# Spacing the buffers of the main pool 2080 instead of 2048 bytes apart, 63 of them instead of 64

## The chip, the cores and the metric

The kernel runs on one core of a Trainium2 chip. The metric is the device time of one execution in microseconds (us), the median over runs. All data are float32; the matmuls of the large products read them in the float32r form.

## What is computed

One decoder layer on 512 tokens of width 2048. Cut to what matters here:

```python
mod = (silu(c) @ w_ada + b_ada)                      # six vectors: shift, scale, gate, twice
h = rmsnorm(x, g_norm_mix) * (1 + sc1) + sh1
q, k, v, xr, xg = split(h @ w_in)                    # 8 heads of 128; two LRU parts of 1024
o_attn = stick_breaking_attention(q, k, v)           # strictly causal, by log-space running sums
o_lru = rg_lru(causal_conv(xr)) * gelu(xg)
y = concat(rmsnorm(o_attn), rmsnorm(o_lru)) @ w_out
x = x + gt1 * y
h = rmsnorm(x, g_norm_mlp) * (1 + sc2) + sh2
hid = square(relu(h @ w_mlp_in))                     # 2048 -> 8192
x = x + gt2 * (hid @ w_mlp_out)                      # 8192 -> 2048
return rmsnorm(x, g_norm_final)
```

## The kernel before, in words

**Precision.** Each float32 operand of a large product is split in two: a float32r copy (high) and the difference (low). A product is then three matmuls into the same PSUM bank: high weight by high activation, high weight by low activation, low weight by high activation (`mm3`, L258 to L263; the same three written out at L1099 to L1101 and L470 to L472). ScalarE makes the high part (L244, L1063, L1069), VectorE the low part (`low`, L121 and L122).

**Operands of a matmul.** In `mm(out, w, a)` the weight tile is the stationary operand, 128x128, loaded afresh for every matmul, and the activation is the moving operand, 512 or 256 columns of 4 bytes. The value product of the attention (`v_mm`, L470 to L472) has it the other way round: the activation is stationary, and a slice of the weight tile moves.

**Stages.** (1) The projections of the recurrence (xr), while the adaLN rows are computed on VectorE from a stream of `w_ada`; (2) q, k and v, with attention, convolution, gates and scans run beside the matmuls in small steps; (3) xg, and the output projection; (4) both MLP products, as one level of a Strassen-like scheme (`strassen`, from L1080): seven products of 256-column operands per set, each 6 matmuls, with the sums of weights made by VectorE (L1057, L1064, L1065) and the sums of activations prepared ahead; (5) the last 512 output columns in plain form, and the final norm.

**What sets the order.** The program is recorded by a framework that schedules it. Priorities (`URGENT`, `EVAC` and others) and the time at which a buffer is expected to come free decide where an instruction stands on its engine, so the number of buffers of a tag takes part in the order. SyncE issues nearly all loads; GpSimd issues the stores of parts, sums and products to DRAM.

**Memory.** Tiles with a tag in `BUFS` come from one pool (`new`, L101 to L104), placed one after the other from low addresses up: constants, `ga`, then `pad` (L140; 40 columns, 160 bytes, used by nothing), `cb` (2 x 4096 bytes), `n` (5 x 2048), `a` (64 x 2048). The constants and `ga` with `pad` end at byte 19968, which is 39 times 512, and every later buffer up to the end of `a` is a multiple of 512 bytes long. So each of them starts at a multiple of 512 bytes. After `a` follow the buffers of the stages on the left side: first `wr`, `wh`, `wl`; in the MLP `w5` and `w3`. Those on the right side (`x` and `tt`; later `ts`, `raw`, `w4`) are placed from the top of the memory down. All of them also start at multiples of 512 in the kernel before.

**What lies in `a`.** Nearly all activations: x, its scaled split, hT (the normalized input, 16 pairs), q, k, v, the parts and sums of the MLP's activations, partial products on their way out, x1 and x2. In the MLP every moving operand is half of an `a` tile (256 of 512 columns), in the plain products a whole one. The weights of the first stage also lie in `a` (`weights1`). In the Strassen stages the stationary operands lie in `w3`, `w4` and `w5`.

Of the kernel before, what the change touches and what calls it, by code (L numbers as in the profile page):

```python
# [16 lines left out]
P = 128  # L17
# [23 lines left out]

URGENT = 150
EVAC = 88
PAD = 40

BUFS = {"cb": 2, "a": 64, "ga": 4, "n": 5}
COLS = {
    "wr": 512, "wh": 512, "wl": 512, "x": 1024, "cb": 1024, "tt": 1280, "n": 512, "a": 512, "ga": 4,  # L50
    "raw": 1024, "ts": 1024, "w3": 768, "w4": 1024, "w5": 1024,
# [13 lines left out]
def hybrid_layer_kernel(  # L65
# [18 lines left out]
    def stage(name):  # L84
        side, tags = STAGES[name]
        for tag in [t for t, (_, _, s) in pools.items() if s == side]:
            del pools[tag]
        region[side].close()
        pool = region[side].enter_context(tc.tile_pool(name=name, bufs=1, reuse_waits="tile", side=side))
        for tag, bufs in tags.items():  # L90
            pools[tag] = pool, bufs, side
            new(tag)
# [3 lines left out]
    count = [0]  # L96

    def T(tag, dt=F32, cols=None):
        return new(next(split_tag) if tag == "w4" else tag, dt, cols)

    def new(tag, dt=F32, cols=None):  # L101
        count[0] += 1
        pool, bufs = (sp, BUFS[tag]) if tag in BUFS else pools[tag][:2]
        return pool.tile([P, cols or COLS[tag]], dt, tag=tag, name=f"{tag}_{count[0]}", bufs=bufs)  # L104

    def bank(tag):
        count[0] += 1
# [2 lines left out]
    def const(cols, name, dt=F32):  # L110
        return sp.tile([P, cols], dt, tag=name, name=name)
# [25 lines left out]
    mods, gm1, spl = (top.tile([P, n], F32, tag=t, name=t) for n, t in ((96, "mods"), (NK, "gm1"), (HEADS, "spl")))  # L137
    region |= {side: ctx.enter_context(ExitStack()) for side in ("right", "left")}
    new("ga")
    const(PAD, "pad")  # L140
    cb = [T("cb"), T("cb")]
# [299 lines left out]
    for o in range(8):  # L441
        t = T("a")
# [805 lines left out]
    for i, (n, ps) in enumerate(parts):  # L1248
# [13 lines left out]
        if n not in left and n < NO - 1:  # L1262
# [10 lines left out]
            with tc.high_priority(offset=SETW):  # L1273
                for k, tok, q in quarters(n, *qs):
                    t = x2[k][:, tok]
# [8 lines left out]
        else:  # L1284
            with tc.high_priority(offset=SETE):
                for j, b in enumerate(bs):
                    t = T("a")
# [14 lines left out]
    for p in final:  # L1302
        t = T("a", F32R)
# [156 lines left out]
```

## Time and profile before

| | |
|---|---|
| median of 3 runs | 2049.47 us (2048.18 to 2051.11) |
| the profiled execution | 2051.77 us |
| its span, first to last instruction | 2050.1 us |
| mean granted TensorE clock | 0.995 |
| TensorE busy | 2009.6 us, 98% of the span, 14,532 matmuls |
| VectorE, ScalarE, GpSimd busy | 1764.0, 1077.8, 181.0 us |
| DMA | 441.45 MB, mean 215 GB/s |

How to read it. A matmul's duration in the profile (283 ns for 256 columns) is longer than its place in the stream, because the next one starts before it ends. What counts is the distance from start to start, called the pace here. It is read from the timeline, or from a window without idle time as its length over the number of matmuls. PE is the matmul side of TensorE, PEld its weight loads. A window's row gives, per engine, busy time and number of instructions, then the granted clock, the share of busy DMA engines and GB/s.

### The profile page before, as it was taken

How to read it: one execution, taken by the hardware profiler on the slowest of the kernel's cores; microseconds unless marked ns; L12 is line 12 of the kernel's file. 1: busy time of each engine (PE TensorE's matmuls, PEld its weight loads, DVE VectorE, ACT ScalarE, POOL GpSimd, SP SyncE). 2: the span in 40 equal slices, each digit the busy share in tenths (PEclk: the TensorE clock that was granted, in tenths of full speed). 3: DMA queues.
4: the chain of work that ended last, by engine and by line, in shares of the span. 5: the costliest groups of instructions: out<-in, count | busy, mean ns of one | idle time of the engine just before them, and what ended most of it. 6: DMA issues, size and time to landing. Idle time of an engine off the chain costs nothing.

```text
span 2050.1 us, 37927 instructions
## 1 busy us (share of the span) xinstructions
PE 2009.6 (98%) x14532; PEld 1904.8 (93%) x14532; DVE 1764.0 (86%) x2971; ACT 1077.8 (53%) x1572; POOL 181.0 (9%) x283
## 2 busy tenths in 40 slices
PE   8999999999999998999999999999999999999997
PEld 6789898778887998999999999999999999999996
DVE  8998776978888699999999999999788778778986
ACT  5443655796423575555555555456455555545542
POOL 0000000000000001221121112100011110210000
PEclk9999999999999999999999999999999999999998
DMA  9896646556789444675566656655485576667644
GB/s 363 303 326 201 200 153 203 167 172 206 226 300 325 134 156 149 213 238 182 185 217 198 194 188 220 211 191 176 148 308 207 210 254 235 232 241 248 237 148 149
DMA packets 205624, 441.45 MB, mean 215 GB/s; under 512 B 20353, under 2 KB 41985, under 8 KB 205442
## 3 DMA queue, kind: packets, MB, share of 16 engines
q1 hardware_dynamic: 178642, 360.78, 53.7%
q0 software_dynamic: 21760, 71.32, 8.9%
q10 hardware_dynamic: 5040, 6.93, 1.0%
q8 instruction: 114, 1.87, 0.4%
q14 instruction: 68, 0.56, 0.1%
HBM read 375.25 MB, written 63.70 MB: 214 GB/s over the span
## 4 chain that ended last, share of the span: by engine, by line
PE 57%; DVE 2%; DMA 1%; issue 0%; ACT 0%; SPq 0%; DVEq 0%
PE ps_mm L1101 9%; PE ps_mm L1100 9%; PE ps_mm L1099 9%; PE ps_z L1101 7%; PE ps_z L1100 7%; PE ps_z L1099 7%; PE ps_o L1101 2%; PE ps_o L1099 2%; PE ps_o L1100 2%; DMA raw<-in_w_mlp_out_dram 1%; DMA a<-x 0%; DVE w L122 0%; DMA a<-sum 0%; DVE a L1346 0%; DVE a L1276 0%
## 5 line engine op out<-in xcount | busy, mean ns | idle before, releaser
L1101 PE MATMUL ps_mm<-a,w 128*128 128x256 f32 x1696 | 479.6, 283 | 1.1 <-DVE w L122 1.1
L1100 PE MATMUL ps_mm<-a,w 128*128 128x256 f32 x1696 | 479.8, 283 | 0.0
L1099 PE MATMUL ps_mm<-a,w 128*128 128x256 f32 x1696 | 479.2, 283 | 0.0
L1063 ACT ACTIVATE w<-raw 128x768 fp32r<-128x768 f32 x244 | 204.9, 840 | 379.0 <-PE ps_mm L1100 165.6
L122 DVE TENSOR_TENSOR w<-ts,w 128x1024 fp32r<-128x1024 f32 x244 | 298.0, 1221 | 116.9 <-PE ps_mm L1100 61.6
L1101 PE MATMUL ps_z<-a,w 128*128 128x256 f32 x1304 | 369.5, 284 | 6.2 <-DVE w L122 6.2
L1099 PE MATMUL ps_z<-a,w 128*128 128x256 f32 x1304 | 369.3, 284 | 0.0
L1100 PE MATMUL ps_z<-a,w 128*128 128x256 f32 x1304 | 369.2, 284 | 0.0
L1101 PEld LDWEIGHTS ps_mm<-a,w 128*128 128x128 f32 x1696 | 325.5, 192 | 1.4 <-DVE w L122 1.4
L1100 PEld LDWEIGHTS ps_mm<-a,w 128*128 128x128 f32 x1696 | 325.7, 192 | 0.2 <-DVE a L122 0.2
L1099 PEld LDWEIGHTS ps_mm<-a,w 128*128 128x128 f32 x1696 | 325.5, 192 | 0.1
L1069 ACT ACTIVATE w<-ts 128x1024 fp32r<-128x1024 f32 x244 | 258.2, 1058 | 113.4 <-DVE ts L1065 101.9
L122 DVE TENSOR_TENSOR w<-raw,w 128x768 fp32r<-128x768 f32 (+1 forms) x296 | 267.4, 904 | 34.3 <-ACT w L244 23.4
L1101 PEld LDWEIGHTS ps_z<-a,w 128*128 128x128 f32 x1304 | 250.6, 192 | 7.1 <-DVE w L122 7.0
L1099 PEld LDWEIGHTS ps_z<-a,w 128*128 128x128 f32 x1304 | 250.8, 192 | 0.1
L1100 PEld LDWEIGHTS ps_z<-a,w 128*128 128x128 f32 x1304 | 250.7, 192 | 0.1
L244 ACT ACTIVATE wh<-wr 128x512 fp32r<-128x512 f32 (+1 forms) x184 | 113.0, 618 | 152.2 <-PE ps_mm L262 65.8
L259 PE MATMUL ps_mm<-a,wh 128*128 128x512 f32 x448 | 176.2, 393 | 3.1 <-ACT wh L244 1.4
L263 PE MATMUL ps_mm<-a,wl 128*128 128x512 f32 x448 | 175.1, 391 | 0.4 <-DVE wl L122 0.2
L262 PE MATMUL ps_mm<-a,wh 128*128 128x512 f32 x448 | 174.7, 390 | 0.0
L1057 DVE TENSOR_TENSOR ts<-raw 128x512 f32<-128x512 f32 x244 | 166.6, 683 | 3.5 <-DMA raw<-in_w_mlp_out_dram 2.4
L122 DVE TENSOR_TENSOR wl<-wr,wh 128x512 fp32r<-128x512 f32 (+1 forms) x184 | 123.7, 675 | 33.3 <-ACT wh L244 32.8
(332 smaller groups left out, 4167.0 us busy)
## 6 DMA issues: line engine op xcount, KB each, us to landing
raw<-in_w_mlp_out_dram SPq DMA_DIRECT2D x124, 512.0 KB, 4.0
raw<-in_w_mlp_in_dram SPq DMA_DIRECT2D x120, 512.0 KB, 3.9
x<-in_w_adaT_dram SPq DMA_DIRECT2D x108, 512.0 KB, 5.7
wr<-in_w_in_dram SPq DMA_DIRECT2D x160, 256.0 KB, 3.4
tt<-in_w_adaT_dram SPq DMA_DIRECT2D x52, 512.0 KB, 6.5
part<-a POOLq DMA_DIRECT2D x84, 256.0 KB, 3.9
a<-part SPq DMA_DIRECT2D x84, 256.0 KB, 6.0
prod<-a POOLq DMA_DIRECT2D x63, 256.0 KB, 5.9
```

The lines of the kernel that those rows point to most:

```text
L122: tt(out=out, in0=full, in1=f32(high), op=ALU.subtract)
L244: act(h[:, :n], r[:, :n], AF.Copy)
L259: first = mm(out, wh, ah, start=start, stop=False, **kw)
L262: mm(out, wh, al, start=False, stop=False, **kw)
L263: mm(out, wl, ah, start=False, stop=stop, **kw)
L1057: tt(out=t[:, : 2 * HT].rearrange("p (a b) -> p a b", a=2), in0=r[:, HT : 3 * HT].rearrange("p (a b) -> p a b", a=2), in1=r[:, q_(0)].unsq ...
L1063: act(h, r[:, HT:], AF.Copy)
L1069: act(h, t, AF.Copy)
L1099: mm(out, wh[:, blk(i)], ah, start=st, stop=False, **kw)
L1100: mm(out, wh[:, blk(i)], al, start=False, stop=False, **kw)
L1101: mm(out, wl[:, blk(i)], ah, start=False, stop=j == js[-1], **kw)
```

## The change

A buffer of the tag `a` is made 8 columns (32 bytes) longer, and only its first columns are handed out; there are 63 of them instead of 64.

```diff
-PAD = 40
+PAD, SKEW = 40, 8
...
-BUFS = {"cb": 2, "a": 64, "ga": 4, "n": 5}
+BUFS = {"cb": 2, "a": 63, "ga": 4, "n": 5}
...
     def new(tag, dt=F32, cols=None):
         count[0] += 1
         pool, bufs = (sp, BUFS[tag]) if tag in BUFS else pools[tag][:2]
-        return pool.tile([P, cols or COLS[tag]], dt, tag=tag, name=f"{tag}_{count[0]}", bufs=bufs)
+        n = cols or COLS[tag]
+        t = pool.tile([P, n + SKEW * (tag == "a")], dt, tag=tag, name=f"{tag}_{count[0]}", bufs=bufs)
+        return t[:, :n] if tag == "a" else t
```

2080 is 4 x 512 + 32, so the k-th buffer starts at 32k modulo 512: all sixteen multiples of 32 occur, each in 3 or 4 buffers. 63 x 2080 = 131,040 bytes, 32 fewer than 64 x 2048 = 131,072. The buffers that follow on the left side (`wr`, `wh`, `wl`; `w5`, `w3`) therefore all start at 480 modulo 512. `x`, `tt`, `ts`, `raw` and `w4` stay where they were, at multiples of 512, as do `cb` and `n` below `a`.

The line numbers of the new kernel are 2 higher from `new` on. Each engine has as many instructions as before. In a handful of places the order changes, since a buffer of `a` is expected at another time.

ScalarE, where the attention of the third pair of heads starts (`tt_770` is the score tile of its first head; `a_801` and `a_805` are the convolution's outputs, `wh_...` high parts of weights). Before:

```order
L552 ACTIVATE a_782_3879<-a_252_1034,vec_63 128x512
L552 ACTIVATE a_801_3990<-a_253_1036,vec_63 128x512
L552 ACTIVATE a_805_4015<-a_254_1038,vec_63 128x512
L244 ACTIVATE wh_787_3893<-wr_786_3891 128x512
L635 ACTIVATE tt_770_3801<-ps_z_767_3786 128x512
L635 ACTIVATE tt_770_3801<-ps_z_768_3787 128x512
L635 ACTIVATE tt_770_3801<-ps_z_769_3788 128x256
L636 ACTIVATE tt_770_3801<-tt_770_3801 128x1280
```

Now:

```order
L554 ACTIVATE a_782_3879<-a_252_1034,vec_63 128x512
L637 ACTIVATE tt_770_3801<-ps_z_767_3786 128x512
L554 ACTIVATE a_801_3990<-a_253_1036,vec_63 128x512
L246 ACTIVATE wh_787_3893<-wr_786_3891 128x512
L637 ACTIVATE tt_770_3801<-ps_z_768_3787 128x512
L246 ACTIVATE wh_793_3942<-wr_792_3940 128x512
L637 ACTIVATE tt_770_3801<-ps_z_769_3788 128x256
L554 ACTIVATE a_805_4015<-a_254_1038,vec_63 128x512
```

The first step of the scores moved ahead of two of the three convolution steps, and a weight's high part came between. VectorE and TensorE are reordered around the same place, with the same instructions.

SyncE, late in the MLP's second product (`a_3824` to `a_3827` are the four residual tiles of output group 1, `n_...` the stored combination of the last group, `raw_...` weights). Before, where the third of the four is loaded:

```order
L1270 DMA a_3824_23287<-x1_4_6544 128x512
L1270 DMA a_3825_23289<-x1_5_6545 128x512
L1270 DMA a_3826_23291<-x1_6_6546 128x512
L1055 DMA raw_3804_23117<-in_w_mlp_out_dram 128x2x512
L1055 DMA raw_3810_23173<-in_w_mlp_out_dram 128x2x512
```

Now, where it stands, after eight more weight loads:

```order
L1057 DMA raw_3865_23565<-in_w_mlp_out_dram 128x2x512
L1301 DMA n_3904_23832<-y_0_15805 128x512
L1301 DMA n_3905_23833<-y_1_15806 128x512
L1272 DMA a_3826_23291<-x1_6_6546 128x512
L1301 DMA n_3906_23834<-y_2_15807 128x512
L1272 DMA a_3827_23293<-x1_7_6547 128x512
L1301 DMA n_3907_23835<-y_3_15808 128x512
```

The third residual tile is loaded ten places later, two ahead of the fourth, and the weight loads that followed it moved up.

## The prediction

> **What bounds the kernel now.** I read the page first, then the stretches of the span as windows, then the timeline of TensorE.
>
> ```profile
> span 2050.1 us, 37927 instructions
> PE 2009.6 (98%) x14532; PEld 1904.8 (93%) x14532; DVE 1764.0 (86%) x2971; ACT 1077.8 (53%) x1572; POOL 181.0 (9%) x283
> ...
> PE 57%; DVE 2%; DMA 1%; issue 0%; ACT 0%; SPq 0%; DVEq 0%
> ```
>
> TensorE is busy for 98% of the span, and it is nearly alone in the chain that ended last. A busy share does not say how fast the matmuls follow each other, so the windows come next.
>
> ```profile
> core 0: us, PE busy (x) PEld busy (x) DVE busy (x) ACT busy (x) POOL busy (x), PEclk, DMA share, GB/s
> 0.00:80.00 80.00, 70.91 (x290) 55.83 (x291) 70.51 (x141) 37.83 (x60) 1.03 (x6) 1.00 0.98 360
> 360.00:400.00 40.00, 37.52 (x169) 30.42 (x168) 37.21 (x64) 29.16 (x46) 0.00 (x0) 0.96 0.58 179
> 560.00:600.00 40.00, 40.00 (x178) 33.11 (x177) 39.93 (x76) 13.78 (x23) 0.00 (x0) 1.00 0.81 266
> 840.00:1880.00 1040.00, 1040.00 (x8662) 1039.50 (x8661) 916.78 (x1479) 546.64 (x720) 140.31 (x226) 1.00 0.63 212
> 1960.00:1980.00 20.00, 18.85 (x157) 18.65 (x156) 17.52 (x29) 12.13 (x19) 0.00 (x0) 1.00 0.60 190
> 2006.00:2050.00 44.00, 30.51 (x228) 28.29 (x226) 31.37 (x70) 11.11 (x24) 0.00 (x0) 0.88 0.48 163
> ```
>
> From 840 to 1880 us, half of the kernel, TensorE does not idle at all at full clock: 8,662 matmuls of 256 columns in 1040.00 us, 0.1201 us each. The wide ones (512 columns, 560 to 600 us) fill 40 us with 177, so 0.226 us each. The difference, 0.106 us for 256 more columns, is 0.414 ns a column, and what a matmul takes beyond its columns is 0.1201 - 0.106 = 0.014 us, the same for both widths. Over 14,532 matmuls that fixed part is 203 us. In such stretches neither DMA (0.63) nor VectorE (917 of 1040 us) sets the time. Only the pace does, and one nanosecond on every matmul is 14.5 us, 0.7% of the kernel.
>
> **What the change can touch.** It removes one buffer of 64, adds no instruction, and moves the addresses of `a` and of what follows it on the left side.
>
> ```profile
> L1101 PE MATMUL ps_mm<-a,w 128*128 128x256 f32 x1696 | 479.6, 283 | 1.1 <-DVE w L122 1.1
> L1101 PE MATMUL ps_z<-a,w 128*128 128x256 f32 x1304 | 369.5, 284 | 6.2 <-DVE w L122 6.2
> L1101 PE MATMUL ps_o<-a,w 128*128 128x256 f32 x416 | 118.0, 284 | 0.4 <-DVE w L122 0.4
> L259 PE MATMUL ps_mm<-a,wh 128*128 128x512 f32 x448 | 176.2, 393 | 3.1 <-ACT wh L244 1.4
> L470 PE MATMUL ps_mm<-wh,a 128*128 128x256 f32 x128 | 36.5, 285 | 0.3 <-DVE a L460 0.3
> ```
>
> Each of these lines stands for one of three matmuls of the split. The Strassen stages alone read `a` as the moving operand 3 x (1696 + 1304 + 416) = 10,248 times, the plain wide products on `ps_mm` 3 x 448 = 1,344 times. Fifteen of sixteen such reads will start off a multiple of 512 bytes, where now none does. A read of 256 columns is 1024 bytes long: from an aligned start it covers exactly two pieces of 512 bytes, from any other start it touches three. The stationary operands in `w3` and `w5` move too, all to 480 modulo 512, those in `w4` stay at 0. In L470 it is `wh` and `wl` that move, at one offset, 480, not sixteen.
>
> **The pace.** No read in the trace of before starts off a multiple of 512, so the price is bounded by the places where the pace departs from 0.120 and 0.226 us without a semaphore in sight.
>
> ```profile
> 1414.39 0.28 PE L1101 MATMUL ps_mm<-a,w 128*128 128x256 f32 x1
> 1414.51 0.28 PE L1099 MATMUL ps_mm<-a,w 128*128 128x256 f32 x1
> ...
> 1415.34 0.28 PE L1100 MATMUL ps_mm<-a,w 128*128 128x256 f32 x1
> 1415.46 0.37 PE L1099 MATMUL ps_z<-a,w 128*128 128x256 f32 x1
> ```
>
> Here, after a wait, nine matmuls start within 1.07 us, 0.1189 us each: 1.1 ns less than the steady pace. So part of the 14 ns is not a law of the array; it depends on how the streams stand to each other in time.
>
> ```profile
> 289.77 0.40 PE L259 MATMUL ps_o<-tt,a 128*128 128x512 f32 x1
> 290.01 0.40 PE L262 MATMUL ps_o<-tt,a 128*128 128x512 f32 x1
> 290.25 0.40 PE L263 MATMUL ps_o<-tt,a 128*128 128x512 f32 x1
> ...
> 291.00 0.29 PE L259 MATMUL ps_o<-tt,a 128*128 128x256 f32 x1
> 291.13 0.28 PE L262 MATMUL ps_o<-tt,a 128*128 128x256 f32 x1
> ```
>
> And here, where widths change, wide ones stand 0.24 us apart (14 ns more) and a narrow one 0.13 (10 ns more), again with no wait. The price of a shifted start therefore lies between -1.1 and +14 ns a matmul by what the rows show; that the whole fixed part of 14 ns falls away is the outermost bound below. One more touched piece of 512 bytes costs nothing where the pieces are whole, since four of them carry the same fixed part as two. It can cost up to a new start, 14 ns, where the first is a fragment. I take +2 ns: nearer the locked pace, because 8,662 matmuls in a row with all their different buffers hold 0.1201 us, so the stream is robust against nearly everything, and on the positive side because a read that begins in the middle of a piece gives the array less per piece and nothing back. It is the weakest number here. The term: 14,532 x 15/16 x 2 ns = 27 us; its bounds are -15 us (-1.1 ns) and, at the slow rows, +190 us, of which I use +4 ns, 54 us, as the far end for a mean over sixteen offsets, some of which should cost nothing.
>
> The Trainium skill (TensorE: Matmul & The Clock Gate, section Back-to-back issue gap) gives a warm gap of N/2.4 + 2.5 ns, 109.2 ns for 256 columns. The trace disagrees, 120.1 ns; if the shifted starts brought the page's gap, the estimate would be 14,532 x 10.9 ns = 158 us less, 1893 us.
>
> **The DMAs of `a`.** Stores out of `a` now start at odd places of the memory, and loads land there.
>
> ```profile
> part<-a POOLq DMA_DIRECT2D x84, 256.0 KB, 3.9
> prod<-a POOLq DMA_DIRECT2D x63, 256.0 KB, 5.9
> sum<-a POOLq DMA_DIRECT2D x56, 256.0 KB, 4.2
> ```
>
> These 203 stores take 4 to 6 us each and lie in the stretch with no idle TensorE and DMA engines at 0.63: they cost nothing, and would only show if the share went near 1. In the first 80 us it is at 0.98 already, and TensorE idles 80 - 70.91 = 9.1 us. The weights loaded there land in `wr`, now at 480. Between 0 and a doubling of that idle time, +9 us, I take +1. If the DMAs were slower, the weights' buffers would come late and their splits with them.
>
> The Trainium skill (DMA: Bandwidth & Descriptors, section How a descriptor splits into AXI transactions) says that a descriptor that doesn't start 256-byte aligned needs an extra transaction. It speaks against the change; no run here shows it, and by it a row of 2048 bytes would take 9 transactions for 8, an estimate of an eighth, which the share of 0.63 absorbs.
>
> **One buffer fewer, and the order.** ScalarE's scores now go ahead of two convolution steps, and TensorE's and VectorE's rows follow. That is at about 375 us; in 360 to 400 TensorE loses 40 - 37.52 = 2.5 us, so the price is between -2.5 and about the same upward; the steps are the same and I take 0. The waiting score step is what is queued ahead on ScalarE then, with the high parts `wh` behind it. On SyncE the third residual tile of group 1 moves ten places back.
>
> ```profile
> 1966.82 4.00 DMA a<-x
> ...
> 1971.35 1.27 DVE a L1276 x3
> ...
> 1973.22 1.15 DVE w L122
> 1974.41 0.39 PE ps_mm L1101
> ```
>
> The fourth of these loads is on the chain already: it lands after 4.00 us, VectorE's in-order queue holds the residual additions (L1276) and behind them a weight's low part (L122) for which TensorE waits; 20 - 18.85 = 1.15 us are lost in that stretch. With two loads issued there instead of one it is one more landing in the worst case, +4 us, none in the best; +0.5. The last 44 us, where TensorE idles 13.5 us at short dependent steps, are not reordered on SyncE: 0.
>
> **Sum.** On the profiled execution's own time: 2051.8 + 27 + 1 + 0.5 = 2080. That execution lies 2.3 us above the median of the three runs, 2049.5, so 2078 us for the median. A measurement of this kernel can tell about 0.2%, 4 us, from no change.
>
> **The rivals.** *No effect on the pace* (chance 0.24). The steady 0.1201 us holds whatever VectorE, ScalarE and DMA do beside it, and over buffers all over the memory; if the matmul reads its operand at a rate that no start address changes, only the small terms are left: 2045.4 to 2053.6. For it: constancy. Against it: that a fixed part of 14 ns exists which is not columns, and that it is 1.1 ns smaller after a wait. The Trainium skill (SBUF — State Buffer, section Who interferes with whom) says that "PE and ACT never wait on anyone", which is this rival; the constant pace agrees with it.
>
> *Faster: the weight load and the moving operand no longer start at the same place* (0.26). Now both start at a multiple of 512 bytes, and the load of the next weights goes on beside the running matmul, from the same phase.
>
> ```profile
> L1099 PEld LDWEIGHTS ps_mm<-a,w 128*128 128x128 f32 x1696 | 325.5, 192 | 0.1
> ...
> L262 PEld LDWEIGHTS ps_mm<-a,wh 128*128 128x128 f32 x448 | 84.2, 188 | 16.1
> ```
>
> A weight load takes 192 ns beside narrow matmuls and 188 beside wide ones. If those 4 ns are a collision of two streams that meet at the same offset, sixteen offsets against two (0 and 480) would leave it in about one of sixteen or eight cases. The price is between -1.1 ns (the pace after a wait; -15 us, 2034) and -4 ns (-55 us, 1995), likeliest -2: 2022. Against it: the wide ones have the same fixed part of 14 ns without those 4 ns. VectorE does not stand in the way, 917 us of work in a stretch that would shrink to 1023. It decides from -0.3 ns on, where the gain exceeds 4 us. That most of the fixed part goes with it (up to -14 ns, -190 us, 1859) gets 0.02 of the 0.26, since no row shows a pace near 0.106 us.
>
> *The change not doing what it says*: 63 buffers 2080 bytes apart do reach all sixteen offsets, each in 3 or 4 buffers. Only the attention's value products are left out, as said. No chance of its own.
>
> **How the numbers follow.** Slower by the pace has 0.50, with +0.3 to +4 ns its own range is 2054 to 2104; its likeliest is 2078. No effect 0.24. Faster 0.26. The range 2020 to 2110 leaves out about a tenth below (the faster case beyond -2.2 ns) and a tenth above (beyond +4.3 ns, towards the slow rows). The chances of faster, same and slower are those of the three cases.
>
> **What would show it.** Right: in 840 to 1880 us fewer matmuls, about 8,530, still with no idle time, starts no longer evenly spaced but going with the buffer, and the wide ones slower by as many nanoseconds. Wrong on the sign: more than 8,662 in that window, with weight loads nearer 188 ns. Wrong on the mechanism: 0.1201 us again, and a difference, if any, in the first 80 us (DMA share, idle time), around 375 us, or at the residual loads near 1967 us.

## The result and the profile after

The changed kernel takes 2040.12 us (median of 6 runs, 2038.38 to 2043.25), the kernel before, beside it, 2049.48 us (6 runs, 2046.46 to 2053.08). The ratio is 0.9956, with a 95% interval of 0.9943 to 0.9969: faster by 0.44%, 9 us. The forecast was 2078 us, slower. The time lies in the range, since the range took in the rival "faster"; the direction was wrong.

The profiled execution took 2041.91 us with a span of 2040.2. Its page begins:

```profile
span 2040.2 us, 37961 instructions
...
PE 1997.6 (98%) x14532; PEld 1884.1 (92%) x14532; DVE 1763.7 (86%) x2971; ACT 1080.9 (53%) x1572; POOL 180.9 (9%) x283
```

TensorE has lost 12.0 us of busy time (2009.6 to 1997.6) at the same 14,532 matmuls. VectorE, ScalarE and GpSimd did not change by more than 3.1 us. The stretches, with the columns of the windows of before:

```profile
0.00:80.00 80.00, 72.52 (x292) 56.40 (x293) 71.11 (x141) 38.20 (x61) 0.94 (x6) 1.00 0.98 363
360.00:400.00 40.00, 37.98 (x171) 30.88 (x170) 37.17 (x64) 28.82 (x45) 0.00 (x0) 0.96 0.59 186
560.00:600.00 40.00, 40.00 (x174) 32.45 (x173) 39.93 (x75) 13.16 (x22) 0.00 (x0) 1.00 0.76 256
840.00:1880.00 1040.00, 1038.17 (x8772) 1036.93 (x8771) 928.40 (x1497) 554.12 (x728) 145.99 (x236) 1.00 0.64 216
1960.00:1980.00 20.00, 18.69 (x156) 18.42 (x155) 19.47 (x31) 9.32 (x12) 0.00 (x0) 1.00 0.51 171
```

Two rows carry the result, with opposite signs. In 840 to 1880 us TensorE does 8,772 matmuls of 256 columns for 8,662 before, although it now idles 1.83 us. In 560 to 600 us it does 174 where 178 stood: the wide ones have become slower. How regular the narrow ones are, the timeline of TensorE shows (start, duration):

```profile
1499.75 0.28 PE L1103 MATMUL ps_z<-a,w 128*128 128x256 f32 x1
1499.87 0.28 PE L1101 MATMUL ps_z<-a,w 128*128 128x256 f32 x1
1499.99 0.28 PE L1102 MATMUL ps_z<-a,w 128*128 128x256 f32 x1
1500.10 0.28 PE L1103 MATMUL ps_z<-a,w 128*128 128x256 f32 x1
...
1501.98 0.28 PE L1101 MATMUL ps_mm<-a,w 128*128 128x256 f32 x1
```

They stand 0.11 to 0.13 us apart, no longer an even 0.12. Taken over all starts of the trace within runs of one width (steps over 130 ns, and over 245 ns between wide ones, are left out as waits), the mean from start to start was, and is:

| | narrow, 256 columns | wide, 512 columns |
|---|---|---|
| matmuls in the program | 12,096 | 2,228 |
| before, ns | 119.90 | 227.37 |
| after, ns | 118.06 | 231.81 |
| difference x matmuls, us | -1.84: -22.3 | +4.44: +9.9 |

The two terms make -12.4 us. The spans differ by 2050.1 - 2040.2 = 9.9 us, so some 2.5 us went back into waits, most of it (1.83 us) in 840 to 1880.

### The profile page after: what moved, and what is told of

The parts are those of the page before. It is cut to its first block, busy times and chain, and to the rows that moved or that the text cites. A ratio compares the mean times of both kernels' runs of the same rounds, so it can differ in the third digit from the quotient of the medians.

```text
span 2040.2 us, 37961 instructions
## 1 busy us (share of the span) xinstructions
PE 1997.6 (98%) x14532; PEld 1884.1 (92%) x14532; DVE 1763.7 (86%) x2971; ACT 1080.9 (53%) x1572; POOL 180.9 (9%) x283
## 5 line engine op out<-in xcount | busy, mean ns | idle before, releaser
L1101 PEld LDWEIGHTS ps_mm<-a,w 128*128 128x128 f32 x1696 | 319.4, 189 | 2.9 <-issue 2.9
L1103 PEld LDWEIGHTS ps_mm<-a,w 128*128 128x128 f32 x1696 | 319.5, 189 | 1.6 <-DVE w L124 1.5
L1102 PEld LDWEIGHTS ps_mm<-a,w 128*128 128x128 f32 x1696 | 319.5, 188 | 0.3 <-DVE a L124 0.2
L1103 PEld LDWEIGHTS ps_z<-a,w 128*128 128x128 f32 x1304 | 245.8, 189 | 7.4 <-DVE w L124 7.3
L1101 PEld LDWEIGHTS ps_z<-a,w 128*128 128x128 f32 x1304 | 246.2, 189 | 1.4 <-issue 0.7
L1102 PEld LDWEIGHTS ps_z<-a,w 128*128 128x128 f32 x1304 | 246.0, 189 | 0.3
L246 ACT ACTIVATE wh<-wr 128x512 fp32r<-128x512 f32 (+1 forms) x184 | 113.4, 618 | 165.6 <-PE ps_mm L264 76.3
```

The source lines that it names most:

```text
L246: act(h[:, :n], r[:, :n], AF.Copy)
L1101: mm(out, wh[:, blk(i)], ah, start=st, stop=False, **kw)
L1102: mm(out, wh[:, blk(i)], al, start=False, stop=False, **kw)
L1103: mm(out, wl[:, blk(i)], ah, start=False, stop=j == js[-1], **kw)
```

## The experiments

Three questions were open: whether the addresses or the smaller count of buffers did it; whether it is the variety of offsets that helps, or the relation of one operand's place to the other's; and why the two widths answer with different signs. "Difference" below means the start of the moving operand minus the start of the stationary one, modulo 256 bytes.

**Only the count of buffers.** The same 63 buffers, 2048 bytes apart:

```diff
-PAD, SKEW = 40, 8
+PAD, SKEW = 40, 0
```

> 63 buffers of 2048 bytes, all starting at multiples of 512 as before: the order of the change without its addresses. Theory A (addresses set the pace): narrow matmuls back at 0.1201 us (8,662 in 840 to 1880 us), wide ones at 0.226, the time within 3 us of the kernel before, 2047 to 2053. Theory B (the count of buffers and the order bring the gain): about 2040, and still 0.120 us a narrow matmul.

Measured: 2049.91 us, ratio 1.0004 (0.9996 to 1.0013), with 119.90 and 227.34 ns. By their traces, TensorE, VectorE, ScalarE and GpSimd each run the same instructions here in the same order as in the changed kernel. The missing buffer and the altered order are worth nothing. It is the addresses.

**The stationary operand instead.** The 32 bytes go to the weight tiles, the buffers of `a` stay at multiples of 512:

```diff
-        t = pool.tile([P, n + SKEW * (tag == "a")], dt, tag=tag, name=f"{tag}_{count[0]}", bufs=bufs)
-        return t[:, :n] if tag == "a" else t
+        t = pool.tile([P, n + SKEW * (tag in ("w3", "w4", "w5"))], dt, tag=tag, name=f"{tag}_{count[0]}", bufs=bufs)
+        return t[:, :n]
```

> 63 aligned buffers of a, but the stationary operands of the MLP (w3, w4) lie 32 bytes further apart than their size, eleven offsets in all; the moving operands all start at multiples of 512, and so do both operands of the wide products. Theory A1 (what matters is that starts differ from matmul to matmul, whichever operand it is): narrow ones at about 0.118 us as in the changed kernel, wide ones back at 0.226, so about 10 us less than the changed kernel, 2030. Theory A2 (the moving operand's own offset matters): narrow ones at 0.1201, about 2049.

Measured: 2040.61 us, ratio 0.9959 (0.9947 to 0.9970), wide 227.30 ns. A window of TensorE alone (length, busy, matmuls, clock, DMA share, GB/s):

```profile
1480.00:1880.00 400.00, 400.00 (x3367) 1.00 0.68 242
```

That is 118.8 ns a narrow matmul. (The mean of steps up to 130 ns is 118.56 here, but it leaves out 257 steps of 131 to 140 ns in which TensorE does not idle. With them it is 118.85. The changed kernel has 26 such steps, and 118.10 with them.) No moving operand left its place, and more than half of the narrow gain, 1.05 of 1.80 ns, came all the same. So the moving operand's own alignment is not what counts. The wide ones, which don't use these tiles, kept their pace. The 2030 us expected for equal gains were missed by the part of the narrow gain that did not come.

**One place for all of `a`.** No variety in `a`: every buffer of it starts 32 bytes beyond a multiple of 512, `w3`, `w5` and the wide stationary tiles too, only `w4` at 0:

```diff
-PAD, SKEW = 40, 8
+PAD, SKEW = 48, 0
```

> 63 buffers of a all at 32 modulo 512 (pad of 48 columns), w3, w5, wh and wl there too, w4 at 0: an odd start, but nearly the same for all. Theory A1 (variety): the narrow pace close to 0.1201, the wide one at 0.226, about 2049. Theory A2 (a start off a multiple of 512 is itself dearer or cheaper): narrow ones near 0.118 and wide ones near 0.232 as in the changed kernel, about 2040. Theory A3 (what counts is whether moving and stationary start at the same offset): only matmuls with w4 change.

Measured: 2034.04 us, ratio 0.9923 (0.9910 to 0.9936), better than the change. Two windows of TensorE alone:

```profile
560.00:600.00 40.00, 40.00 (x178) 1.00 0.79 263
...
1480.00:1880.00 400.00, 400.00 (x3390) 1.00 0.69 248
```

The same stretch of 400 us holds 3,336 matmuls before and 3,388 after the change. Here it holds 3,390, 118.0 ns each, without any variety in `a`. And the 178 wide ones are back: each has difference 0 (32 and 32). So the moving operand need not vary. The narrow pairs still take two differences in turn, 0 with `w3` and `w5` and 32 with `w4`, so variety of the difference is not excluded by this run alone; the next one does that.

**The pace by itself.** A kernel that leaves the whole layer out and runs series of 60 equal matmuls, with nothing else to do, over offsets of the moving operand (`ma`) and the stationary one (`wa`), counted from the starts of the two tiles, which lie a multiple of 512 bytes apart:

```
mm(ps[:, :n], w[:, wa : wa + P], a[:, ma : ma + n], start=i == 0, stop=i == REPS - 1)
```

> Leaves out the whole layer: 96 series of 60 matmuls one after the other with all operands resident, no semaphore between them, nothing on the other engines; 256 columns and 512, moving operand at each of the 16 offsets with aligned weights, weights at each offset with aligned moving operand, both equal, two offsets in turn, random ones. Its time has no meaning beside the layer's. Theory A1 (variety): every series with one constant pair of offsets stands at one pace, 120 ns and 227 ns; series with changing offsets at about 118 and 232 ns. Theory A2: a table that depends on the moving offset alone, equal in constant and in changing series. Theory A3: depends on the difference of the two offsets, with 0 special. If the pace of 120 ns comes from the other engines' accesses, it does not appear here at all.

Windows that run from just before the 11th start of a series to just before its 60th, which is 49 steps (the count also takes in what is still running at the edges). In order: narrow with the moving operand at 192 and 256 bytes, the stationary one at 0; narrow with random places for both; wide with the moving operand at 0, 32 and 256 bytes, and wide at random:

```profile
57.20:62.75 5.55, 5.55 (x51) 1.00 0.00 0
71.15:77.03 5.88, 5.88 (x51) 1.00 0.00 0
341.44:347.22 5.78, 5.78 (x51) 1.00 0.01 3
356.82:367.93 11.11, 11.11 (x50) 1.00 0.01 1
370.49:381.92 11.43, 11.43 (x50) 1.00 0.00 0
468.25:479.36 11.11, 11.11 (x50) 1.00 0.01 1
995.68:1007.05 11.37, 11.37 (x50) 1.00 0.00 0
```

Divided by 49: narrow 113.3, 120.0 and 118.0 ns; wide 226.7, 233.3, 226.7 and 232.0 ns. The eight differences in steps of 32 bytes give:

| difference, bytes | 0 | 32 | 64 | 96 | 128 | 160 | 192 | 224 |
|---|---|---|---|---|---|---|---|---|
| narrow, ns | 120.0 | 117.8 | 117.8 | 120.1 | 118.7 | 117.4 | 113.3 | 118.3 |
| wide, ns | 226.7 | 233.3 | 228.9 | 233.4 | 233.4 | 234.3 | 233.3 | 233.3 |

The narrow row is with the stationary operand at 0; the same difference 192 made by a stationary operand at 64 gave 117.8. Equal starts give 120.0 and 226.7 wherever they lie (32, 96, 256 or 416), and a difference of 256 bytes acts as 0. A constant difference of 192 is the fastest of all the series here, so it is not variety that helps. Two things more are answered. The mean over the eight is 117.9 for narrow and 232.1 for wide, and the changed kernel, which mixes all eight, has 118.06 and 231.81. Two places in turn do not always give the mean of the two: the moving operand at 0 and 480 in turn came to 116.7 ns, below the 120.0 and 118.3 of each alone. And difference 0, where every pair of the kernel before stood, is the best place for a wide matmul and one of the worst for a narrow one.

**The wide ones alone.** A gap tile of 32 bytes shifts `wr`, `wh` and `wl`, nothing else:

```diff
-PAD, SKEW = 40, 8
+PAD, SKEW = 40, 0
+GAPS = {'front': 8}
...
+        gap = lambda: pool.tile([P, GAPS[name]], F32, tag="gap", name=f"gap_{name}", bufs=1)
+        if name in GAPS and side == "left":
+            gap()
```

> Only wr, wh and wl lie at 32 modulo 512, a at 0, the MLP's operands all at multiples of 512: the wide half of the change alone. Theory D: narrow ones at 120 ns except the value products (moving wh, stationary a: 117.8), the wide ones with wh or wl at 233.3 instead of 226.7: some 1,700 x 6.6 ns less 768 x 2.2 ns, 10 us more than before, about 2059. If wide matmuls do not care, about 2048.

Measured: 2054.64 us, ratio 1.0031 (1.0020 to 1.0041), the wide ones with `wh` and `wl` at 233.28 ns, the narrow ones without the value products at 119.91.

```profile
560.00:600.00 40.00, 40.00 (x173) 1.00 0.75 253
...
1480.00:1880.00 400.00, 400.00 (x3336) 1.00 0.66 237
```

Only the wide row moved, 178 to 173. The loss on the wide matmuls is a part of its own, 0.0031 x 2049.5 = 6 us here, less than 1,776 matmuls with `wh` or `wl` x (233.28 - 227.37) = 10 us. Of the other 4 us some 2 come back in the attention's 768 value products, whose moving operand is `wh` or `wl`: they went to 116.98 ns. The rest was not traced.

**Difference 192 in the layer.** All of `a` and the wide stationary tiles at 192, the narrow ones' at 0 (so wide keep difference 0):

```diff
-PAD, SKEW = 40, 8
+PAD, SKEW = 88, 0
+GAPS = {'mlp': 16}
```

> Theory D (the pace goes by the difference of the moving and the stationary start, modulo 256 bytes): a, wr, wh, wl all at 192 modulo 256, w3, w4, w5 at 0. The plain wide products have difference 0, so 0.2267 us; the Strassen stages and the plain narrow ones have 192, where the table has 113.3 ns: 11,000 x 6.6 ns = 73 us less than with all aligned, about 1977. Rival: VectorE, which needs 106 ns a matmul in that stretch, becomes the bound or makes TensorE wait for weights, then the pace lies between and the time at 1985 to 2010. Rival: the 117.8 ns that the table shows when the same difference is made by moving the stationary operand: about 2025.

Measured: 2025.45 us, ratio 0.9885 (0.9855 to 0.9915), the fastest of all kernels in the study. Its six runs fall into two groups, 2012.43 to 2020.11 and 2030.79 to 2032.65. The profiled execution (span 2010.7) shows why:

```profile
840.00:1000.00 160.00, 156.63 (x1350) 154.11 (x1349) 154.93 (x276) 84.74 (x112) 29.03 (x43) 1.00 0.64 205
1040.00:1400.00 360.00, 359.85 (x3051) 359.03 (x3051) 348.15 (x586) 201.31 (x269) 50.47 (x74) 1.00 0.61 201
1480.00:1880.00 400.00, 397.89 (x3508) 397.49 (x3507) 334.21 (x492) 219.79 (x294) 50.38 (x93) 1.00 0.73 262
```

From 1480 on a matmul takes 397.89 / 3,508 = 113.4 ns, from 1040 to 1400 it takes 118.0. The same starts have two paces, and the stream stays in one for hundreds of microseconds. VectorE, busy for 348.15 of 360 us in the slower stretch, does not set that pace: of the 3,049 steps there 2,943 lie at 116 to 120 ns one by one, not at 113 with waits between. In the first row the next bound shows: VectorE is busy 154.93 of 160 us, and TensorE waits 3.4.

**The same difference, made by the weights.** `w3`, `w4`, `w5` at 64, `a` at 0:

```diff
-PAD, SKEW = 40, 8
+PAD, SKEW = 40, 0
+GAPS = {'mlp': 16, 'sums': 48}
...
+        if name in GAPS and side == "right":
+            gap()
```

> The same difference of 192 as with a at 192 and w3, w4, w5 at 0, made the other way: a at 0, w3, w4, w5 at 64 modulo 256. If only the difference counts: 113.3 ns, about 1977. If the table's second value for it holds (117.8 ns with the stationary operand moved): 11,000 x 2.2 ns less, about 2025.

Measured: 2031.41 us (2014.51 to 2032.73), ratio 0.9894 (0.9864 to 0.9923). The profiled execution (span 2030.7) is mostly in the slower pace:

```profile
1480.00:1880.00 400.00, 400.00 (x3398) 1.00 0.69 249
```

117.7 ns, where the run before had 113.4, at the same difference. From 840 to 880 us, without a wait, its steps are 113.3 ns: this layout has both paces too.

**Finer steps, and other widths.** Series again, in steps of 8 bytes:

> Leaves out the whole layer: series of 60 matmuls with resident operands. Difference of the starts in steps of 8 bytes for 256 columns, of 16 for 512, in steps of 32 for 384 and 128 columns; and the difference of 192 made from eleven pairs of starts, each after a series at difference 0 or after a wide series. If the difference alone counts, all eleven stand at 113.3 ns; if there are two stable states, those with the moving operand ahead (192 and 0) at 113.3 and (0 and 64) at 117.8, and the series before may decide. The time has no meaning beside the layer's.

In order: narrow at 8, 104 and 112 bytes, and a series of 128 columns:

```profile
22.07:27.95 5.88, 5.88 (x51) 1.00 0.01 3
107.78:114.16 6.38, 6.38 (x51) 1.00 0.00 0
115.43:120.98 5.55, 5.55 (x51) 1.00 0.00 0
931.58:937.05 5.47, 5.47 (x51) 1.00 0.00 0
```

120.0, 130.2, 113.3 and 111.6 ns. Odd multiples of 8 bytes give 118.4 to 130.2, most of them 120.0; 16 and 32 bytes 116.7 (32 had 117.8 in the table); 112 and 192 bytes 113.3. Pairs of 128 columns took 111.6 to 111.7 ns at every difference tried: half the columns at almost the best pace of 256. At 384 columns the spread was 173.3 to 176.8 ns. Of the wide series, 240 bytes reached the 226.7 of 0. Difference 192 was made from eleven pairs of starts in 22 series: 12 stood at 113.3 ns, 10 at 117.8.

**What came before, and whose start counts.** Fifteen differences, each behind three wide series and three waits; then series in which the difference is kept to the pair's own stationary operand, the next one, or the one after, while the places change at random:

> Leaves out the whole layer; its time has no meaning. First part: fifteen differences of the starts (16 to 240 bytes), each after three wide series of different length and after three waits for ScalarE. If there are two stable states at some differences, the six series of one difference stand at two paces; differences with one state stand at one. Second part: series in which the stationary start changes at random from matmul to matmul and the moving start follows it, with a constant difference to the matmul's own stationary operand, to the next one's, or to the one after. If the pace is set by the running matmul's reads against the load of the next weights, the wide series with difference 0 stands at 226.7 ns only for 'next', and at about 232 for the two others; if by a matmul's own operands, only for 'own'; if starts as such matter, for none.

In order: 112 behind a wide series; 192 behind two wide series, with the stationary operand at 0 and at 96, and behind a wait, with it at 32; a narrow series with difference 0 to its own stationary operand, at random places:

```profile
505.10:510.65 5.55, 5.55 (x51) 1.00 0.01 3
990.63:996.40 5.77, 5.77 (x51) 1.00 0.01 3
1005.62:1011.18 5.56, 5.56 (x51) 1.00 0.00 0
1032.82:1038.38 5.56, 5.56 (x51) 1.00 0.01 3
1308.86:1314.64 5.78, 5.78 (x51) 1.00 0.01 3
```

At 112 the steady pace was 113.3 in all six. At 192 it was 117.8 or 113.3: the two paces seen in the layer. What came before and the place differ together between these series; the last run separates them. 192 is not alone in this: of the fifteen differences eight held one pace over their six series, and seven (16, 80, 116, 128, 160, 192 and 200) took two or more, 16 bytes from 113.3 to 118.7. And when the places change from pair to pair, no relation helps: all nine narrow series came to 117.9 to 118.9 ns (the last 40 of the 60), all six wide ones to 231.1 to 232.9, even those with difference 0 to their own operand. So none of these three relations alone sets a pair's pace, and the steady paces of the table were seen only in series of pairs that stand alike.

**112 in the layer, for the narrow ones only.** Longer weight tiles, their contents 16 bytes in, 62 buffers of `a`:

```diff
-BUFS = {"cb": 2, "a": 63, "ga": 4, "n": 5}
+BUFS = {"cb": 2, "a": 62, "ga": 4, "n": 5}
+GAPS = {'mlp': 32, 'sums': 32}
...
+        if tag in ("w3", "w4", "w5"):
+            return pool.tile([P, n + 64], dt, tag=tag, name=f"{tag}_{count[0]}", bufs=bufs)[:, 4 : n + 4]
```

> The three tags of weight tiles that the 256-column pairs load (w3, w4, w5) start 128 bytes beyond a multiple of 256, and their contents 16 bytes further, so that every one of those 11,160 matmuls has its moving start 112 bytes (mod 256) above its stationary start; all wide matmuls keep difference 0, and there are 62 buffers of a. Theory (the pace is set by the difference of the two starts): 113.3 ns a narrow pair whatever came before, as in the series by themselves, and 227.4 ns a wide one: 2050 - 11,160 x (119.9 - 113.3) = 1976 us, and up to 15 us more where VectorE (542 of 560 us busy in 840 to 1400 us of the run with a at 192) makes TensorE wait: 1975 to 1992. Rival (in the layer the pairs fall back to the slower of two states as they did at 192): 117.8 ns in most stretches, about 2025 us. Rival (spread is what helps, not a chosen difference): no better than the 2040 of the change.

Measured: 2058.28 us, ratio 1.0040 (1.0025 to 1.0055).

```profile
1480.00:1880.00 400.00, 400.00 (x3335) 1.00 0.67 237
```

119.9 ns, not 113.3: the theory of the difference alone missed by 80 us.

**Its control.** The same tiles and count with difference 0 (no `GAPS`, `[:, :n]`):

> The same longer weight tiles and the same 62 buffers of a, but with every start back at difference 0 and no gap tiles: the control of the run before it. Theory: 119.9 ns and 227.4 ns as in the kernel before, 2050 us within 0.2%; the padding and the two missing buffers are worth nothing. Rival (the missing buffers or the longer weight tiles move the time themselves): over 0.2% off.

Measured: 2058.14 us, ratio 1.0044 (1.0031 to 1.0057). So the 9 us come from the 62 buffers or the longer tiles (which of the two was not taken apart), and difference 112 brought nothing at all.

**The place within 32 bytes.** In the kernel with 112, the stationary operand stood 16 bytes off a multiple of 32; in the series it had been the moving one. Series over 22 pairs of starts:

> No layer: series of 60 narrow pairs as before, 22 pairs of starts, each behind two wide series, two waits, and two waits with ScalarE and VectorE busy beside it (14 copies and 14 additions). The kernel with difference 112 ran at 120.0 ns in the layer, where the stationary tile started 16 bytes beyond a multiple of 32 and the moving one on it; the series that gave 113.3 had it the other way round. Theory D1 (the start of each operand within its own 32 bytes counts, not the difference alone): moving at 112, 144, 176 or 240 with stationary on a multiple of 32 gives 113.3, stationary at 144, 176, 160 or 16 with 112 less... that is, moved off the multiple itself, gives 117 to 120, with nothing else busy. Theory D2 (only the difference counts, and in the layer the other engines' reads or what came before hold the pairs in a slower state): all ten pairs with difference 112 give 113.3 behind w and s, and 117 to 120 with the other engines busy. Difference 192 by six pairs: 113.3 or 117.8 by what came before, as in the two series before. Difference 32 by (32, 0) and (0, 224): 116.7 both; (16, 240): 116.7 by D2, another by D1. Difference 0 at 16 and 80: 120.0 by both.

In order, each pair written as (moving, stationary): difference 112 as (112, 0), (0, 144) and (16, 160); 192 as (208, 16); 0 as (16, 16) and (0, 0):

```profile
20.29:25.85 5.56, 5.56 (x51) 1.00 0.02 3
397.55:403.43 5.88, 5.88 (x51) 1.00 0.00 0
689.64:695.20 5.56, 5.56 (x51) 1.00 0.00 0
1007.53:1013.08 5.55, 5.55 (x51) 1.00 0.00 0
1462.36:1468.07 5.71, 5.71 (x51) 1.00 0.00 0
1538.93:1544.81 5.88, 5.88 (x51) 1.00 0.01 3
```

113.5, 120.0, 113.5, 113.3, 116.5 and 120.0 ns. With the moving operand 16 bytes off a multiple of 32 and the stationary one on it, difference 112 was fast in all five pairs of starts; the other way round it took 116.7 to 120.0 in all five. The kernel in the layer stood the other way round, and had the pace of that form. At difference 192 the three pairs with both operands 16 bytes off, (208, 16), (16, 80) and (112, 176), were fast behind everything, as was (96, 160); (0, 64) was slow behind everything, and (192, 0) alone went by what came before: 117.8 behind both wide series, 113.3 behind all four waits. Difference 32 took 116.7 to 118.4 by its three pairs. Against both theories, difference 0 at 16 and at 80 was not 120.0 but 116.7 or 118.3. ScalarE and VectorE ran their extra work mostly ahead of the series they were meant for, so that half of the test says little; with (112, 0) ScalarE was busy throughout, and the pace was at 113.3 once settled.

## Why the prediction was wrong

**What bounds the kernel: right.** The pace of TensorE alone decides. 840 to 1880 us gained 110 matmuls, and waits changed by 2 us.

**The price of a shifted start: the step that failed.** It said "I take +2 ns: nearer the locked pace", on the positive side "because a read that begins in the middle of a piece gives the array less per piece and nothing back", and its term was "14,532 x 15/16 x 2 ns = 27 us". The two widths together measured -12.4 us. Two things in it are wrong. The reason looks at the moving operand alone; the shift of the weights by itself brought more than half of the gain (118.85 ns), and equal starts at other multiples of 32 have the 120.0 of the aligned ones. Nor do pieces of 512 bytes show: a moving operand that starts 256 bytes into one has the aligned pace in both widths, 120.0 and 226.7. And one price was used for both widths: the runs have -1.84 ns for 12,096 narrow and +4.44 ns for 2,228 wide ones. For the wide ones the sign was right by luck: what they lose is the equal starts, at which they are fastest. The prediction read the constancy of 0.1201 us over "all their different buffers" as robustness against nearly everything. It was the constancy of one cause: all those buffers had difference 0. A series at difference 0 has exactly 120.0 with nothing else running, and a stream held at one setting says nothing of its neighbours. One row did speak: the nine steps after a wait, 118.9 ns from rounded starts, are 118.0 by the trace's nanoseconds, so the bound of -1.1 ns was too small; why they are shorter stays open.

**The rival "faster": the right two operands, with one price for two widths.** That the pace hangs on how the weight load and the moving operand start to each other is what the runs show, and its likeliest price, -2 ns, is near the narrow one's. That they collide where they "start at the same place" is not shown: difference 96 is as slow as 0 (120.1), and equal starts are the best for wide ones. The sign it named came true, in the groups of weight loads after:

```profile
L1102 PEld LDWEIGHTS ps_mm<-a,w 128*128 128x128 f32 x1696 | 319.5, 188 | 0.3 <-DVE a L124 0.2
...
L264 PEld LDWEIGHTS ps_mm<-a,wh 128*128 128x128 f32 x448 | 84.2, 188 | 18.0
```

192 ns beside narrow matmuls became 188, what wide ones always had. But these 4 ns are not the price: in the narrow series a weight load takes 192 ns at difference 0 and 188 at both 96 and 192, where the pace is 120.1 and 113.3. What was held against the rival, that the wide ones have the same fixed part without those 4 ns, could have been read as a sign that the widths differ. With the two measured prices its sum becomes 2051.8 - 22.3 + 9.9 - 2.3 = 2037.

**No effect** falls: the start does change the rate. The Trainium skill (SBUF — State Buffer, section Who interferes with whom) says that PE waits on no other engine, and the series agree with it: 120.0 ns with all others idle, as in the full layer. But it was cited for a constant pace, and the dependence here is between TensorE's own two operands. The Trainium skill's gap of N/2.4 + 2.5 ns (TensorE: Matmul & The Clock Gate, section Back-to-back issue gap) is 109.2 for 256 columns, and that page gives it for an isolated matmul, not for a stream of pairs; no series with such pairs came under 113.3, and the formula has no term for the starts.

**The small terms: right, and near zero.** DMAs of `a`: +1 us was taken; TensorE's idle time in the first 80 us went from 9.1 to 7.5 us at the same share of 0.98, and in 840 to 1880 the share is 0.64 for 0.63. The shifted stores did become a little dearer: the packets of GpSimd's queue took 9.3% of the span (190 us) for 8.9% of it with 63 aligned buffers (182 us), and 9.5 and 9.6% where all of `a` lay at 32 or 192. That is 4 to 6% more time, less than the estimated eighth, and TensorE did not wait for it. One buffer fewer: 0 was taken, and 63 aligned buffers gave 2049.91. Around 375 us TensorE's busy time is 37.98 of 40 for 37.52; at the residual loads 18.69 of 20 for 18.85.

**What stays open.** Why 256 bytes are the period, why 16 bytes in the moving start act otherwise than the same 16 in the stationary one, and why difference 192 and others have two paces. The runs show that these are so, in series with nothing else running, not what inside the chip makes it so.

## What to carry to other kernels

Where TensorE runs without idle time, divide a window by its matmuls for each width, and try the start of the moving operand against that of the stationary one as a setting of its own: it was worth 6% of a narrow pair and 3% of a wide one here, with opposite best values, and costs a few bytes of padding, as long as no buffer has to go for it (62 buffers with longer weight tiles cost 9 us). Choose one pair of places and keep it for every pair in a run (all of `a` at 192 and the weights at 0 gave 2025 us); spreading over all offsets only buys the mean. Measure the pair in the layer: difference 112, fast in the series, brought nothing there with the 16 bytes on the weights' side. And a pace that nothing disturbs may be constant because every operand stands alike, so it is no evidence on what another layout does.

## What was not expected of the hardware

- The step from one narrow pair to the next ranged from 113.3 to 130.2 ns by the two starts alone, at full clock with all other engines idle; wide pairs from 226.7 to 234.7.
- Two steady paces, 113.3 and 117.8 ns, for the same starts (192 and 0), chosen by what ran before in the series, and in the layer, where the choice was not traced, kept for hundreds of microseconds: 118.0 in 1040 to 1400 us, 113.4 in 1480 to 1880. That kernel's runs took 2012 to 2020 or 2031 to 2033 us.
- With places changing at random from pair to pair, the pace is the mean (117.9 to 118.9 and 231.1 to 232.9 ns) whether a pair's own difference, or that to one of the next two stationary operands, is held constant.
- Pairs of 128 columns follow each other every 111.6 ns, hardly faster than 256 columns at the best difference.
